# One core, a hybrid mLSTM and band attention trunk: column sums spread out, a weight split put behind the sums of the piece in front of it, one output group for all rows at once

## The chip, the cores and the metric

The kernel runs on one core of a Trainium2 chip. The metric is the device time of one execution in microseconds (us). Before the change the median of three runs is 2637.78 us (2635.75 to 2638.52).

## What is computed

One batch of 512 tokens of width 2048 goes through two layers. `mod` below is a product of a conditioning vector with wide matrices, one column at a time; the kernel makes each column by one pass over a 128x2048 tile (a "column sum", tile `ada`).

```python
# layer 1: mLSTM, 8 heads (q, k: 256 wide; v, o, z: 512 wide)
mod = silu(c) @ ada_w + ada_b                      # shift, scale, gate
h = rmsnorm(x) * (1 + scale) + shift
qk = silu(causal_conv(h @ w_qk))                   # 4 taps
v, o, z, gates = h @ w_v, h @ w_o, h @ w_z, h @ w_g + gate_b
ht = mlstm(q, k, v, log input gate, log forget gate)   # decays exp(...) times q k^T, times v
y = sigmoid(o) * rmsnorm(ht) * silu(z)
x = x + gate * rmsnorm(y @ a_w_out)
# shared keys and values, then layer 2: 16 heads of 128, band of 9 chunks of 64
k, v = (rmsnorm(x) * (1 + kscale) + kshift) @ kv_w
q, z = (rmsnorm(x) * (1 + scale) + shift) @ b_w_in
x = x + gate * rmsnorm((softmax(q k^T + bias) v * silu(z)) @ b_w_out)
```

## The kernel before

**Products.** All is float32. A product of two float32 tiles is made as three TensorE products of rounded halves: hi by hi, hi by lo, lo by hi (`mm3`, L314). Weights come from memory as one stream of pieces in the order of use, mostly 128x1024 (512 KB), into three tiles `wr` by SyncE's queue (`raw_load`, L253). Each piece is split into `wh`: hi is a cast on ScalarE, lo a subtraction on VectorE (`split`, L242, all on line L243). Three such pairs of tiles exist, so a split can be at most about two pieces ahead of TensorE.

**Seven products.** In the later parts two by two blocks are multiplied by seven products in place of eight (`proj_s`, L358, and `proj_v`, L422). For a piece this needs sums of its blocks: three VectorE instructions (L282, L283, L284; L283 writes into `wr` itself) make `ws`, which is split into `wsh` in the same way as `wh`. So such a piece costs VectorE three sums and two subtractions, and ScalarE two casts. `proj_v` makes the values of heads 3 to 7 (TensorE tiles `ps_dv`, `ps_cv`, `ps_av`, `ps_ev`; eight pieces each), the column groups 2 and 3 of the first half of `a_w_out`, and one group of the values of `kv_w`. The tile scheduler sets the order on each engine from priorities (`tc.high_priority`), and a small helper `behind` (L235) can force one instruction behind another on its engine.

**Stages.** The start and the columns needed first (0 to about 155 us); heads 0, 1 and 2 of the mLSTM; heads 3 to 7, each about 165 us, all alike; `a_w_out` in two halves of its rows; `kv_w`; 16 heads of the band attention; the last product. In heads 0 to 2 VectorE has 57 column sums to make besides its splits, scheduled by `background(n)` (L683): it sums the n oldest loaded tiles and refills up to three (two from one pool, one from another). Their 1 MB loads are issued by GpSimd's queue, which also carries the short row transfers `dsc` (`row_out`, L883) and the factors `f` of the heads. In `a_w_out`, further column sums ("whole", L1092 to L1103) are loaded by SyncE's queue between weight loads, two or three at a time.

**Head 0 to 2.** The convolution (`conv`, L787) works in 128x512 tiles tagged "t" of a pool of three, `tp`. Many others use this pool: `g32` of the gates, the squares `sq` of the norm (L1053), and the row that `row_out` sends to memory. The gates (`gates`, L747) are a chain of small VectorE steps that ends in `ssum` (L773), which TensorE waits for (`ps_at`, L782). The scores of a head (`scores`, L847) multiply `qk` tiles into `ps_s`, and multiply by decays that ScalarE makes with exp (L859, L861); silu of the convolution is L800. The two functions are in different tables of ScalarE, and a change of table is an instruction of its own, `ACT_TABLE_LOAD`.

**a_w_out, second half.** `rows(g, ms, ...)` makes column group g (512 columns) for the row blocks ms. Group 0 is made for all four row blocks of 128 tokens at once, groups 1 to 3 for two pairs of row blocks in turn, so that the weights of these groups are streamed twice. In the second pair the residual and the normed rows of the first pair are made (`residual`, `turned`, `key_inputs`).

**Band attention.** Eight pairs of k-tiles are multiplied by seven products, and their inputs need sums (`input_sums`, L1364, `three_sums`, L498), which VectorE makes before head 0 starts.

Of the kernel before, what the change touches and what calls it, by code (L numbers as in the profile page):

```python
# [29 lines left out]
SHIFTS = 9  # L30
# [17 lines left out]
ATT_PAIRS = 8  # L48
BANKS = ("pppp", "paaa")
# [54 lines left out]
def stream():  # L104
# [50 lines left out]
    tile_b("a_w_out", 0, KT)  # L155
    for _ in PAIRS:
        for g in range(1, 4):
# [8 lines left out]
    for h in range(BH):  # L166
        tile_s("b_w_in", h * P, D + h * P, ATT_PAIRS, True)
# [20 lines left out]
def hybrid_trunk(ctx, tc, xT, xN, c, adaT, cols, wst, wg, ext, kc, out):  # L188
# [73 lines left out]
    def wpiece(mat, groups=(), pl=None, bufs=(2, 2), early=False):  # L262
# [9 lines left out]
        with tc.high_priority(ahead[0]):  # L272
# [25 lines left out]
            parted[:] = split(hi, lo, raw, *first[1:] if i < 3 else ())  # L298
            out = [(hi, lo)]
            for j, t in enumerate(ts):  # L300
# [3 lines left out]
                split(sh, sl, t)  # L304
# [28 lines left out]
    def proj_a(mat, xs, ps, t0=0, t1=S):  # L333
        proj(mat, xs, [ps], 8, 0, len(xs), len(xs) - 1, t0, t1)
# [23 lines left out]
    def proj_s(mat, xs, ss, f, z1, z2, name, pl, bufs, at={}, merged=False, banks="pppp", lead=AHEAD):  # L358
# [4 lines left out]
        pieces = pair_pieces(f, merged)  # L363
        begun = set()
        h0, h1_ = slice(0, 256), slice(256, 512)
        for i, (sk, nk) in enumerate(pieces):
# [55 lines left out]
    def proj_v(mat, xs, ss, zs, name, pl, bufs, at={}):  # L422
# [41 lines left out]
        out = []  # L464
# [211 lines left out]
    loaded = []  # L676
# [6 lines left out]
    def background(n):  # L683
# [4 lines left out]
        while pending and len(loaded) < 3:  # L688
            p, bufs = (bp, 1) if len(pending) % 3 == 1 else (ap_, 2)
# [3 lines left out]
    for n, step in enumerate(steps):  # L693
        if n > len(steps) - 6:
# [38 lines left out]
    ahead[0] = AHEAD  # L733

# [12 lines left out]
    def gates():  # L747
# [4 lines left out]
        g32 = tp.tile([P, S], F32, tag="t", name="g32")  # L752
# [34 lines left out]
    def conv(ps, ch, name, lead, woven):  # L787

        acc = tp.tile([P, S], F32, tag="t", name=f"cv_{name}")
        with tc.high_priority(lead):  # L790
            if woven:
                rows = tp.tile([P, S], F32, tag="t", name=f"cu_{name}")
# [90 lines left out]
    def row_out(h, i, ps, f):  # L883

        r = tp.tile([P, S], F32, tag="t", name=f"row{h}_{i}")[0:1]
# [35 lines left out]
    for h in range(NH):  # L921
# [4 lines left out]
        for i in range(4):  # L926
# [6 lines left out]
            else:  # L933
                ps = newp(f"ps_qk{h}_{i}")
                proj_a("a_w_in", h1, ps)
            qk.append(conv(ps, chs[i], f"{h}_{i}", AHEAD if h == HALF else 100 if h > HALF and i > 1 else 0, h in (0, HALF)))
            if 1 < h <= HALF:
                background(2)
# [9 lines left out]
        if h == 0:  # L948
            background(2)
# [31 lines left out]
        for i in (2 * h, 2 * h + 1):  # L981
            pin(nc.sync.dma_start(bsc[i], ext[i].partition_broadcast(P)))
        if h == 0:
            for j in range(4):
# [14 lines left out]
        if h < HALF:  # L999
            background(2 + (h == 0))  # L1000
        if h:
            so = []
        for i in range(4):
# [26 lines left out]
        if h == 0:  # L1030
            background(2)
# [37 lines left out]
        if h < HALF:  # L1069
            background(3)  # L1070
# [107 lines left out]
    xrs = [[] for _ in range(4)]  # L1178
# [530 lines left out]
```

## Time and profile before

| what | value |
|---|---|
| median of three runs | 2637.78 us (2635.75 to 2638.52) |
| the profiled execution's own time | 2635.22 us |
| its span | 2633.4 us |
| mean clock granted to TensorE | 0.997 of full speed |
| TensorE (PE) busy | 2574.4 us, 98% |
| VectorE (DVE) busy | 2335.1 us, 89% |
| ScalarE (ACT) busy | 1428.7 us, 54% |
| moved by DMA | 510.62 MB, mean 194 GB/s |

The span runs from the first to the last recorded instruction; 1.8 us of the profiled execution's time lie around it. Busy TensorE time is not TensorE at its peak: the ends of its instructions are modelled, and they overlap. An idle time stands in brackets in the timeline, with what ended it behind the arrow.

### The profile page before, as it was taken

What the parts mean: (1) busy time and instruction counts of PE and PEld (TensorE: products, weight loads), DVE (VectorE), ACT (ScalarE), POOL (GpSimd) and SP (SyncE); (2) the same over time, 40 slices, a digit from 0 to 9 for tenths busy, and PEclk for the clock granted to TensorE, in tenths of its full rate; (3) what the DMA queues carried; (4) which work ended last, traced back from release to release, by engine and by line L of the source; (5) the groups of instructions that cost most, each with busy time, mean ns of one, the idle gap of its engine ahead of it and who ended that gap; (6) DMA issues with size and microseconds to landing.
All of it is one profiled execution on the core that took longest, in us unless ns stands there. A gap on an engine that the chain in (4) does not pass through costs nothing.

```text
span 2633.4 us, 45758 instructions
## 1 busy us (share of the span) xinstructions
PE 2574.4 (98%) x17994; PEld 2407.5 (91%) x17994; DVE 2335.1 (89%) x3812; ACT 1428.7 (54%) x2106; POOL 59.8 (2%) x118
## 2 busy tenths in 40 slices
PE   8999999999999999999999999999999999999998
PEld 6887787899999999999999898788999899999887
DVE  8978988999989999899998886977997999999767
ACT  4344533466555665556655453578543766776523
POOL 0000111000000000000000000000000000000000
PEclk9999999999999999999999999999999999999999
DMA  9876787533333333333336548988654544444787
GB/s 364 313 265 251 272 329 290 192 108 114 124 102 129 115 111 125 105 125 118 110 130 237 195 150 327 301 259 302 226 179 146 171 130 138 138 130 132 254 299 251
DMA packets 155315, 510.62 MB, mean 194 GB/s; under 512 B 17893, under 2 KB 31749, under 8 KB 140633
## 3 DMA queue, kind: packets, MB, share of 16 engines
q1 hardware_dynamic: 144346, 443.89, 49.6%
q0 software_dynamic: 10752, 63.79, 6.6%
q8 instruction: 141, 2.31, 0.4%
q14 instruction: 76, 0.62, 0.1%
HBM read 473.96 MB, written 38.90 MB: 195 GB/s over the span
## 4 chain that ended last, share of the span: by engine, by line
PE 56%; DVE 25%; DMA 8%; issue 7%; ACT 3%; POOL 0%; SPq 0%; DVEq 0%; ACTq 0%; POOLq 0%
DVE wh L243 6%; PE ps_y L311 5%; PE ps_azo L311 4%; PE ps_czo L311 4%; PE ps_dzo L311 4%; DVE ada L552 3%; PE ps_y_True L311 3%; PE ps_dz L311 3%; PE ps_cz L311 3%; PE ps_y_False L311 3%; PE ps_az L311 3%; DMA wr<-in_wst 3%; DVE wsh L243 2%; PE ps_bzo L311 2%; DVE cv L797 2%
## 5 line engine op out<-in xcount | busy, mean ns | idle before, releaser
L243 ACT CAST wh<-wr 128x1024 fp32r<-128x1024 f32 (+1 forms) x536 | 553.3, 1034 | 473.3 <-DVE wr L283 102.0
L243 DVE TENSOR_TENSOR wh<-wr,wh 128x1024 fp32r<-128x1024 f32 (+1 forms) x536 | 643.3, 1203 | 127.2 <-ACT wh L243 126.3
L243 ACT CAST wsh<-ws 128x768 fp32r<-128x768 f32 (+1 forms) x296 | 241.8, 817 | 298.4 <-PE ps_az L311 67.1
L243 DVE TENSOR_TENSOR wsh<-ws,wsh 128x768 fp32r<-128x768 f32 (+1 forms) x296 | 276.8, 935 | 45.7 <-ACT wsh L243 44.5
L552 DVE CUSTOM_DVE_ANT_0 ada<-ada,scB,cl 128x2048 f32<-128x2048 f32 (+1 forms) x89 | 205.8, 2322 | 11.3 <-DMA ada<-in_adaT 11.2
L282 DVE TENSOR_TENSOR ws<-wr 128x512 f32<-128x512 f32 (+1 forms) x296 | 198.5, 673 | 5.3 <-DMA wr<-in_wst 5.0
L311 PE MATMUL ps_y_False<-wh,y 128*128 128x512 f32 x768 | 168.6, 380 | 2.3 <-DVE wh L243 2.2
L311 PE MATMUL ps_y<-wh,y 128*128 128x512 f32 x768 | 168.6, 380 | 0.1
L311 PEld LDWEIGHTS ps_y_False<-wh,y 128*128 128x128 f32 x768 | 144.3, 189 | 24.4 <-DVE wh L243 4.2
L311 PEld LDWEIGHTS ps_y<-wh,y 128*128 128x128 f32 x768 | 144.3, 189 | 20.8 <-DVE wh L243 0.5
L311 PE MATMUL ps_kv<-wh,hkv 128*128 128x512 f32 x576 | 127.3, 381 | 1.6 <-DVE wh L243 1.5
L311 PE MATMUL ps_v<-wh,h 128*128 128x512 f32 x576 | 127.3, 380 | 0.0
L311 PEld LDWEIGHTS ps_kv<-wh,hkv 128*128 128x128 f32 x576 | 108.0, 189 | 18.5 <-DVE wh L243 3.3
L284 DVE TENSOR_TENSOR ws<-wr 128x256 f32<-128x256 f32 (+1 forms) x296 | 122.1, 414 | 3.1
L283 DVE TENSOR_TENSOR wr<-ws,wr 128x256 f32<-128x256 f32 (+1 forms) x296 | 121.8, 413 | 2.4
L311 PEld LDWEIGHTS ps_v<-wh,h 128*128 128x128 f32 x576 | 108.3, 189 | 15.8 <-issue 0.9
L311 PE MATMUL ps_l<-h,wh 128*128 128x512 f32 x480 | 107.7, 380 | 2.1 <-DVE wh L243 2.1
L311 PEld LDWEIGHTS ps_l<-h,wh 128*128 128x128 f32 x480 | 90.3, 189 | 16.5 <-DVE wh L243 3.3
L311 PE MATMUL ps_azo<-h,wh 128*128 128x256 f32 (+1 forms) x606 | 92.9, 285 | 0.0
L311 PE MATMUL ps_y_True<-wh,y 128*128 128x512 f32 x384 | 83.3, 379 | 0.0
L311 PEld LDWEIGHTS ps_y_True<-wh,y 128*128 128x128 f32 x384 | 72.5, 189 | 10.2
L311 PEld LDWEIGHTS ps_azo<-h,wh 128*128 128x128 f32 x606 | 79.2, 192 | 1.1
(431 smaller groups left out, 5825.2 us busy)
## 6 DMA issues: line engine op xcount, KB each, us to landing
wr<-in_wst SPq DMA_DIRECT2D x506, 512.0 KB, 3.7
ada<-in_adaT POOLq DMA_DIRECT2D x57, 1024.0 KB, 7.1
ada<-in_adaT SPq DMA_DIRECT2D x49, 1024.0 KB, 7.0
ada<-in_adaT SPq DMA_DIRECT2D x36, 512.0 KB, 6.5
wr<-in_wst SPq DMA_DIRECT2D x26, 384.0 KB, 6.2
xt<-nsc SPq DMA_DIRECT2D x32, 256.0 KB, 3.8
yr<-ysc SPq DMA_DIRECT2D x28, 256.0 KB, 5.4
ysc<-zo SPq DMA_DIRECT2D x24, 256.0 KB, 3.9
```

The source lines that it names most:

```text
L243: ins = nc.scalar.copy(hi, src), nc.vector.tensor_tensor(lo, src, hi.bitcast(F32), op=ALU.subtract)
L282: nc.vector.tensor_tensor(t[:, : 2 * w], r[:, w : 3 * w], r[:, : 2 * w], op=ALU.subtract)
L283: nc.vector.tensor_tensor(r[:, w : 2 * w], t[:, w : 2 * w], r[:, :w], op=ALU.add)
L284: nc.vector.tensor_tensor(t[:, 2 * w :], r[:, 3 * w :], r[:, w : 2 * w], op=ALU.subtract)
L311: product[0] = nc.tensor.matmul(ps, a, b, start=start, stop=stop)
L552: pin(nc.vector.tensor_tensor_reduce(c, c, (sc or scB)[:, j * w : (j + 1) * w], 1.0, mod[:, i : i + 1] if j else col(CB + i), ALU.mult, AL ...
L797: nc.vector.scalar_tensor_tensor(acc[:, d:], ps[:, : S - d], col(CW + 32 * (3 - d) + ch), acc[:, d:], op0=ALU.mult, op1=ALU.add)
```

## The change

The change has seven parts, and nothing else of the kernel is touched.

1. Three column sums fewer are made in heads 0 to 2 (`SHIFTS` 9 to 6); they are made in `a_w_out` with the others there.
2. `background` starts 12 steps before the end of the start and not 6, is called for one sum at a time, also between the two pieces of a projection (`mid`), and gets a fourth tile (`ring`) after the start.
3. For heads 0 to 2 a new pool `ep` gives the convolution, its input copy, `g32` and the row their own tiles, which were tiles of `tp`. The masked decays of head 0 are made behind its values.
4. The transfers of the attention's bias rows (`bsc`) are issued in heads 3 to 7 in place of all heads.
5. In `proj_v` the split of a piece's weights is put behind the splits of the sums of the piece in front of it, ScalarE's behind ScalarE's and VectorE's behind VectorE's (`chain`).
6. In the second half of `a_w_out` column group 1 is made for all four row blocks at once as well, so that eight weight pieces are streamed, cast and subtracted once less. The steps that hung on the three groups of the second pair hang on two.
7. Head 0 of the attention makes six of its eight pairs by seven products and the last two by eight (`ATT_FIRST`); the sums for these two are made in its steps 2 and 3, for the other heads. The products into B are made in two halves of 256 columns.

```diff
-SHIFTS = 9
+SHIFTS = 6
+ATT_FIRST = 6
...
-def pair_pieces(f, merged=False):
+def pair_pieces(f, merged=False, late=False):
...
+    if late:
+        out = [([[a]], [b]) for a, b in zip(sk[f - n :], nk)]
+        return [([sk[i : i + 2]], []) for i in range(0, f - n, 2)] + out
...
     tile_b("a_w_out", 0, KT)
+    tile_b("a_w_out", 512, KT)
     for _ in PAIRS:
-        for g in range(1, 4):
+        for g in range(2, 4):
...
-            parted[:] = split(hi, lo, raw, *first[1:] if i < 3 else ())
+            parted[:] = split(hi, lo, raw, *first[1:] if i < 3 else chain or ())
...
-                split(sh, sl, t)
+                done = split(sh, sl, t)
+                if chain is not None:
+                    chain[:] = done[::-1]
...
+            if mid and ka > k0:
+                mid()
             [(hi, lo)] = wpiece(mat)
...
-                        acc(ps, slice(0, S), main, b0 + 4 * m + 2 * j + t, xs[2 * k + j], False)
+                            for w in (h0, h1_) if late and t else (slice(0, S),):
+                                acc(ps, w, main, b0 + 4 * m + 2 * j + t, xs[2 * k + j][:, :, w], False)
...
-            held.append((k, *wpiece(mat, [2], pl, bufs)))
+            held.append((k, *wpiece(mat, [2], pl, bufs, chain=chain)))
...
-    loaded = []
+    loaded, ring = [], [(ap_, 2), (ap_, 2), (bp, 1)]
...
-        while pending and len(loaded) < 3:
-            p, bufs = (bp, 1) if len(pending) % 3 == 1 else (ap_, 2)
+        while pending and len(loaded) < len(ring):
+            p, bufs = ring.pop(0)
+            ring.append((p, bufs))
...
-        if n > len(steps) - 6:
+        if n > len(steps) - 12:
             background(2 if n % 2 else 0)
...
+    ep = mst.enter_context(pool("t0", side="right"))
+    ring.insert(0, (ep, 1))
...
+    def early_tile(h, tag, bufs, name):
+        return ep.tile([P, S], F32, tag=tag, name=name, bufs=bufs) if h else tp.tile([P, S], F32, tag="t", name=name)
...
-        acc = tp.tile([P, S], F32, tag="t", name=f"cv_{name}")
+        acc = early_tile(early, "cv", 3, f"cv_{name}")
...
-        r = tp.tile([P, S], F32, tag="t", name=f"row{h}_{i}")[0:1]
+        r = early_tile(h < HALF, "row", 2, f"row{h}_{i}")[0:1]
...
-                proj_a("a_w_in", h1, ps)
+                proj_a("a_w_in", h1, ps, lambda: background(1))
...
-        for i in (2 * h, 2 * h + 1):
+        for i in range(BH * (h - HALF - 1) // (NH - HALF - 1), BH * (h - HALF) // (NH - HALF - 1)) if h > HALF else ():
             pin(nc.sync.dma_start(bsc[i], ext[i].partition_broadcast(P)))
...
+    gate_row(0, 1)
+    rows(1, range(4), ys, whole_steps(3, (0, 2, 4, 6, 8, 10, 12)))
     for pair, ms in enumerate(PAIRS):
-        for g in range(1, 4):
+        for g in range(2, 4):
...
-                at = whole_steps(3, (0, 6, 12)) if g < 3 else whole_steps(3, (0,)) | {k: whole_sum for k in (4, 8, 12)}
+                at = whole_steps(3, (0, 6, 12)) if g < 3 else {k: whole_sum for k in (0, 4, 8)}
...
-                    w = slice(0, 256 + 256 * i)
+                    w = slice(0, S if k >= ATT_FIRST else 256 + 256 * i)
                     split(t[:, 0, w], t[:, 1, w], raw[i][:, w])
+                if k >= ATT_FIRST:
+                    plain[k] = raw
+                    h2s.append(None)
+                    continue
...
+    def plain_sums(k):
+        h2s[k] = three_sums(plain[k], kq, f"h2s{k}", ATT_PAIRS, h2[2 * k][:, :, 256:], True)
```

The scheduler turns this into another order of instructions on the engines. Three places follow, of before and of after the change apart. A name such as `wh116` is piece 116 of the weight stream, `ws116_0` its sums, `wsh116_0` the split of the sums; the last number of a name only tells tiles apart.

First place: VectorE in head 3, where the values begin. Rows of `wh` and `wsh` are the subtractions that make lo, `cv_3_2` and `cv_3_3` the convolution of head 3. Before:

```order
L284 TENSOR_TENSOR ws116_0_5471<-wr116_5469 128x256
L797 SCALAR_TENSOR_TENSOR cv_3_2_5270<-zq3_2_0_5033,cl_100,cv_3_2_5270 128x510
L797 SCALAR_TENSOR_TENSOR cv_3_3_5279<-zq3_2_1_5034,cl_100,cv_3_3_5279 128x510
L243 TENSOR_TENSOR wh116_5475<-wr116_5469,wh116_5475 128x1024
L243 TENSOR_TENSOR wsh115_0_5416<-ws115_0_5409,wsh115_0_5416 128x768
L797 SCALAR_TENSOR_TENSOR cv_3_2_5270<-zq3_2_0_5033,cl_100,cv_3_2_5270 128x509
L243 TENSOR_TENSOR wsh116_0_5478<-ws116_0_5471,wsh116_0_5478 128x768
```

After:

```order
L289 TENSOR_TENSOR ws116_0_5460<-wr116_5458 128x256
L813 SCALAR_TENSOR_TENSOR cv_3_2_5259<-zq3_2_0_5022,cl_100,cv_3_2_5259 128x510
L813 SCALAR_TENSOR_TENSOR cv_3_3_5268<-zq3_2_1_5023,cl_100,cv_3_3_5268 128x510
L248 TENSOR_TENSOR wsh115_0_5405<-ws115_0_5398,wsh115_0_5405 128x768
L248 TENSOR_TENSOR wh116_5464<-wr116_5458,wh116_5464 128x1024
L287 TENSOR_TENSOR ws117_0_5528<-wr117_5526 128x512
L248 TENSOR_TENSOR wsh116_0_5467<-ws116_0_5460,wsh116_0_5467 128x768
```

The subtraction of `wsh115_0` stood behind that of `wh116` and now stands ahead of it; a step of `cv_3_2` that stood between the two `wsh` is no longer there.

Second place: ScalarE at the same point of head 3. `cv_3_2` and `cv_3_3` with ACTIVATE are silu, `e3_0` is the first decay (exp), CAST makes hi. Before:

```order
L243 CAST wsh116_0_5478<-ws116_0_5471 128x768
L800 ACTIVATE cv_3_2_5270<-cv_3_2_5270 128x512
L243 CAST qk_3_2_5276<-cv_3_2_5270 128x512
L800 ACTIVATE cv_3_3_5279<-cv_3_3_5279 128x512
L243 CAST wh117_5543<-wr117_5537 128x1024
L243 CAST qk_3_3_5285<-cv_3_3_5279 128x512
L243 CAST wsh117_0_5546<-ws117_0_5539 128x768
L859 ACT_TABLE_LOAD
L859 ACTIVATE e3_0_5530<-nmd3_5289,aT_1513 128x128
```

After:

```order
L248 CAST wh117_5532<-wr117_5526 128x1024
L816 ACTIVATE cv_3_3_5268<-cv_3_3_5268 128x512
L875 ACT_TABLE_LOAD
L875 ACTIVATE e3_0_5519<-nmd3_5278,aT_1534 128x128
L248 CAST wsh117_0_5535<-ws117_0_5528 128x768
L816 ACT_TABLE_LOAD
L816 ACTIVATE cv_3_2_5259<-cv_3_2_5259 128x512
L248 CAST wh118_5601<-wr118_5595 128x1024
L248 CAST qk_3_2_5265<-cv_3_2_5259 128x512
L248 CAST qk_3_3_5274<-cv_3_3_5268 128x512
```

The two silu stood together ahead of the only table load in these rows. Now the first decay stands between them, so that the table is loaded once for exp and once more for silu, and the cast of `qk_3_2` stands behind both loads and behind the casts of `wh117`, `wsh117_0` and `wh118`.

Third place: VectorE at the end of the start. `ada32` to `ada35` are column sums (ISA is the sum's instruction, the row with `mod` alone reads its accumulator), `q1_0` to `q1_3` take products of head 1 out of TensorE's banks. Before:

```order
L243 TENSOR_TENSOR wh32_1203<-wr32_1125,wh32_1203 128x768
L524 SCALAR_TENSOR_TENSOR h1_15_1314<-h1t_15_1315,mod_103,h1_15_1314 128x512
L243 TENSOR_TENSOR gw_1519<-graw_1518,gw_1519 128x16x16
L731 TENSOR_TENSOR q1_0_265<-q1_0_265,ps_l6_6_1183 128x512
L243 TENSOR_TENSOR wh33_1228<-wr33_1153,wh33_1228 128x768
L731 TENSOR_TENSOR q1_1_266<-q1_1_266,ps_l7_6_1208 128x512
L243 TENSOR_TENSOR wh34_1256<-wr34_1181,wh34_1256 128x768
L243 TENSOR_TENSOR wh35_1284<-wr35_1206,wh35_1284 128x768
```

After:

```order
L742 TENSOR_TENSOR q1_0_265<-q1_0_265,ps_l6_6_1189 128x512
L562 ISA ada32_0_1178,mod_103<-ada32_0_1178,scB_123,cl_100 128x2048
L562 ISA mod_103 128x1
L562 ISA ada33_0_1180,mod_103<-ada33_0_1180,scB_123,cl_100 128x2048
L562 ISA mod_103 128x1
L742 TENSOR_TENSOR q1_1_266<-q1_1_266,ps_l7_6_1220 128x512
L248 TENSOR_TENSOR wh33_1240<-wr33_1153,wh33_1240 128x768
L248 TENSOR_TENSOR wh34_1274<-wr34_1187,wh34_1274 128x768
L562 ISA ada34_0_1182,mod_103<-ada34_0_1182,scB_123,cl_100 128x2048
L562 ISA mod_103 128x1
L562 ISA ada35_0_1211,mod_103<-ada35_0_1211,scB_123,cl_100 128x2048
```

Before, the first column sum behind `wh32` came behind `wh38`; now six of them, `ada32` to `ada37`, stand between `wh32` and `wh37`, the first four of them in these rows.

More of the change, by code (lines that the diff above doesn't have):

```diff
@@ L260, in raw_load, with wpiece @@
         loads.append(raw)
-    def wpiece(mat, groups=(), pl=None, bufs=(2, 2), early=False):
+    def wpiece(mat, groups=(), pl=None, bufs=(2, 2), early=False, chain=None):
         if stock and not early:
@@ L356, in proj_b, with proj_s @@
             held.clear()
-    def proj_s(mat, xs, ss, f, z1, z2, name, pl, bufs, at={}, merged=False, banks="pppp", lead=AHEAD):
+    def proj_s(mat, xs, ss, f, z1, z2, name, pl, bufs, at={}, merged=False, banks="pppp", lead=AHEAD, late=False):
         D, C, A, B = [(newa if b == "a" else newp)(f"ps_{n}{name}") for n, b in zip("dcab", banks)]
-        pieces = pair_pieces(f, merged)
+        pieces = pair_pieces(f, merged, late)
         begun = set()
@@ L462, in empty @@
             return z0, z1
-        out = []
+        out, chain = [], []
         for k in range(n):
@@ L1176, in row_rstd @@
         return r
-    xrs = [[] for _ in range(4)]
+    xrs, fetched_xr = [[] for _ in range(4)], [0] * 4
     def fetch_xr(m, n):
-        for g in range(len(xrs[m]), len(xrs[m]) + n):
-            xrs[m].append(xr_p.tile([P, S], F32, tag="xr", name=f"xr{m}_{g}"))
+        for g in range(fetched_xr[m], fetched_xr[m] + n):
+            if m < 3:
+                xrs[m].append(xr_p.tile([P, S], F32, tag="xr", name=f"xr{m}_{g}"))
+            else:
+                if g % 2 == 0:
+                    t = kp.tile([P, 2, S], F32, tag="k", name=f"xr{m}_{g}", bufs=KT)
+                    xrs[m] += [t[:, i, :] for i in range(2)]
             nc.sync.dma_start(xrs[m][g], xN[m, :, g * S : (g + 1) * S])
+        fetched_xr[m] += n
     def residual(m):
@@ L1393, in hybrid_trunk @@
         for g in range(2):
-            turn = {2 + 6 * i: lambda i=i: turned(1, [i], True) for i in range(3)} if pair == 0 and g == 1 else {}
+            turn = {k: lambda i=i: turned(1, [i], True) for i, k in enumerate((4, 8, 14))} if pair == 0 and g == 1 else {}
             if pair == 0 and g == 0:
@@ L1459, in queries @@
         z2 = at.tile([P, 2, 256], F32, tag="z", name=f"z{h}", bufs=2)
-        proj_s("b_w_in", h2, h2s, ATT_PAIRS, z1, z2, f"z{h}", kq, (2, 2), steps, True)
+        proj_s("b_w_in", h2, h2s, ATT_PAIRS if h else ATT_FIRST, z1, z2, f"z{h}", kq, (2, 2), steps, True, late=True)
         zq, sz = (z.rearrange("p a t -> p (a t)") for z in (z1, z2))
@@ L1551, in hybrid_trunk @@
         if h < BH:
-            qs[h], szs[h] = queries(h, {1: turn, 2: mid, 3: end})
+            steps = {1: turn, 2: mid, 3: end}
+            if h == 0:
+                add_at(steps, {2 + i: lambda k=k: plain_sums(k) for i, k in enumerate(plain)})
+            qs[h], szs[h] = queries(h, steps)
+            if h == 0:
+                for k, raw in plain.items():
+                    s1 = h2s[k][0]
+                    split(s1[:, 0, :], s1[:, 1, :], raw[0][:, 256:])
+                tst.close()
         else:
```

59 lines of the change are left out of this document (29 added, 30 removed).

## The prediction

> **What bounds the kernel now.** I read the page first: busy times, then its costliest groups. TensorE is busy for almost the whole span.
>
> ```profile
> PE 2574.4 (98%) x17994; PEld 2407.5 (91%) x17994; DVE 2335.1 (89%) x3812; ACT 1428.7 (54%) x2106; POOL 59.8 (2%) x118
> ...
> L243 ACT CAST wh<-wr 128x1024 fp32r<-128x1024 f32 (+1 forms) x536 | 553.3, 1034 | 473.3 <-DVE wr L283 102.0
> L243 DVE TENSOR_TENSOR wh<-wr,wh 128x1024 fp32r<-128x1024 f32 (+1 forms) x536 | 643.3, 1203 | 127.2 <-ACT wh L243 126.3
> ...
> L311 PE MATMUL ps_y_False<-wh,y 128*128 128x512 f32 x768 | 168.6, 380 | 2.3 <-DVE wh L243 2.2
> ```
>
> The change takes no product away (head 0 of the attention even gets a few more), so it can only take away time in which TensorE waits. The waits of TensorE by what ended them are the budget; these are the rows that the change can touch, out of some 50 us in all.
>
> ```profile
> PE ps_cv L311 <- DVE wsh L243: 9.8, 10, 1.6
> PE ps_q L311 <- ACT sp_q L243: 4.9, 5, 3.8
> PE ps_s L311 <- ACT qk L243: 4.4, 1, 4.4
> PE ps_z L311 <- DVE wh L243: 3.4, 2, 2.7
> ...
> PE ps_y_False L311 <- DVE wh L243: 2.2, 4, 0.8
> ...
> PE ps_dz L311 <- DVE h2s L243: 1.8, 1, 1.8
> PE ps_dz L311 <- ACT h2s L243: 1.7, 1, 1.7
> ...
> PE ps_n L311 <- DVE so L1054: 1.3, 1, 1.3
> ...
> PE ps_at L782 <- DVE ssum L773: 1.2, 1, 1.2
> ```
>
> The columns are the total, the number of waits and the longest. The sum of these rows is 30.7 us, so no version of this change gains much more. The view counts from the modelled end of the last matmul, and that lies late: one of 512 columns is recorded as 380 ns (the page's last row above), but twelve in a row take 2.75 us, so the first and the last start 2.75 less 0.38 us apart, 0.215 us for each.
>
> ```profile
> 161.42 2.75 PE L311 MATMUL ps_lead<-h,wh 128*128 128x512 f32 x12
> ```
>
> So each wait really costs about 0.16 us more than its row. A measurement of this kernel can tell about 0.2%, 5.3 us, from no change.
>
> **Heads 0 to 2 (parts 1 to 3).** Three places wait here, and the timeline shows why. At 315 us the scores of head 1 wait for `qk`, because its convolution began late: ScalarE waited for a row's transfer to give back a tile of `tp`, and VectorE then had column sums between its steps.
>
> ```profile
> 293.79 0.81 ACT L795 ACTIVATE cv<-q,cl 128x512 f32<-128x512 f32 x1 [1.57 <-DMA dsc<-row]
> ...
> 315.09 1.14 PE L311 MATMUL ps_s<-qk,qk 128*128 128x512 f32 x2 [4.37 <-ACT qk L243]
> ...
> 378.90 2.35 DVE L552 CUSTOM_DVE_ANT_0 ada<-ada,scB,cl 128x2048 f32<-128x2048 f32 x1 [2.16 <-DMA ada<-in_adaT]
> ...
> 420.22 0.60 ACT L1053 ACTIVATE sq<-ps_n 128x512 f32<-128x512 f32 x1 [5.69 <-DMA dsc<-row]
> ```
>
> The waits of the stretch from 600 to 1420 us alone tell how much of `ps_q` belongs to later heads:
>
> ```profile
> PE ps_q L311 <- ACT sp_q L243: 1.1, 4, 0.3
> ```
>
> With its own tiles the convolution of head 1 is done long before, ahead of the gates, so the 4.4 us go. What is late next there is `f0`, which waits for GpSimd's transfers, 0 to 2 us of it uncovered; I take 0. Around 385 us `ps_z` waits 3.4 us because VectorE waits for loads of sums; the fourth tile and three sums fewer (3 x 2.35 = 7.1 us of VectorE) should cover that. At 423 us the row's transfer held a tile that `sq` needed for 5.69 us, and TensorE paid 3.8 of it and 1.3 in `ps_n`; rows now have tiles of their own. Together 3.4 + 3.8 + 1.3 = 8.5 us, with 5 as the low end, since sums still crowd there.
>
> Against it stands what these sums displace. They now come first between `wh32` and `wh37`, into time in which VectorE sits idle waiting for TensorE or ScalarE:
>
> ```profile
> 155.77 0.89 DVE L243 TENSOR_TENSOR wh<-wr,wh 128x768 fp32r<-128x768 f32 x1
> ...
> 161.62 0.69 DVE L731 TENSOR_TENSOR q<-q,ps_l 128x512 f32<-128x512 f32 x1 [2.01 <-PE ps_l L311]
> ...
> 166.37 0.96 DVE L243 TENSOR_TENSOR wh<-wr,wh 128x768 fp32r<-128x768 f32 x1 [2.88 <-ACT wh L243]
> 169.39 0.69 DVE L731 TENSOR_TENSOR q<-q,ps_l 128x512 f32<-128x512 f32 x1 [2.06 <-PE ps_l L311]
> ...
> 228.52 0.74 DVE L773 SCALAR_TENSOR_TENSOR ssum<-ps_li,cl,gate_nmd 8x512 f32<-8x512 f32 x1
> ...
> 311.82 0.74 DVE L797 SCALAR_TENSOR_TENSOR cv<-q,cl,cv 128x509 f32<-128x509 f32 x1
> ```
>
> And from the view of the transfers, with the median time to landing at the end:
>
> ```profile
> ada<-in_adaT POOLq DMA_DIRECT2D x57, 1024.0 KB, 7.1
> ```
>
> `wh32` is split at 156.7 and TensorE takes it up at 161.4: a lead of 4.7 us, and two sums are 4.7 us. Pieces behind follow at 18 x 0.215 = 3.9 us, in which VectorE has 1.6 us of other work (a split of 0.9 and one step of 0.7), so the lead grows again by 2.3 us with each piece that has no sum in front of it. It falls to about 1 us or nothing at `wh33` and `wh35`, and is made good by `wh41`. This covers the sums if their loads land in the usual 7.1 us; if each of the three pairs lands 2 us later, TensorE loses 3 x 2 = 6. I take 0.7, with 0 to 6. At the gates, nine convolution steps of head 1 (0.74 us each, 0.66 less their overlap) now stand in front of `ssum`: 6 us more of VectorE's work in that stretch, of which some goes into places where the chain of the gates waits for ScalarE. The wait of 1.2 us becomes about 3: +1.8, between 0 (all of it in such places) and 4. Heads 0 to 2: -4.4 - 8.5 + 0.7 + 1.8 = -10.4.
>
> **Heads 3 to 7 (parts 4 and 5).** Each head waits twice for a `wsh`. The first time, VectorE subtracted `wh116`, which TensorE needed only at 649.63, ahead of `wsh115`, for which TensorE stood idle.
>
> ```profile
> 643.48 1.22 DVE L243 TENSOR_TENSOR wh<-wr,wh 128x1024 fp32r<-128x1024 f32 x1
> 644.62 0.95 DVE L243 TENSOR_TENSOR wsh<-ws,wsh 128x768 fp32r<-128x768 f32 x1
> ...
> 645.62 0.49 PE L311 MATMUL ps_cv<-wsh,h1s 128*128 128x256 f32 x2 [1.56 <-DVE wsh L243]
> ...
> 649.63 0.50 PE L311 MATMUL ps_dv<-wh,h1s 128*128 128x256 f32 x3
> ...
> 654.32 1.46 PE L311 MATMUL ps_s<-qk,qk 128*128 128x512 f32 x6
> ```
>
> The swap saves 644.62 - 643.48 = 1.14 us, and the second wait (9.8 / 5 - 1.56 = 0.4) goes too: 1.54 a head, 7.7 in five. `wh116` then still has 3 to 4 us of lead. But the chain also moves ScalarE, as the second place of the order shows: a load of the table and the first decay come between the two silu, and another load before the second.
>
> ```profile
> 650.38 0.83 ACT L243 CAST wsh<-ws 128x768 fp32r<-128x768 f32 x1
> 651.23 1.28 ACT L859 ACT_TABLE_LOAD   x1
> 652.53 0.40 ACT L859 ACTIVATE e<-nmd,aT 128x128 f32<-128x128 f32 x1
> ```
>
> A switch costs 651.21 to 652.53, 1.32 us. From the page, the means of VectorE's sums and subtractions:
>
> ```profile
> L243 DVE TENSOR_TENSOR wsh<-ws,wsh 128x768 fp32r<-128x768 f32 (+1 forms) x296 | 276.8, 935 | 45.7 <-ACT wsh L243 44.5
> L282 DVE TENSOR_TENSOR ws<-wr 128x512 f32<-128x512 f32 (+1 forms) x296 | 198.5, 673 | 5.3 <-DMA wr<-in_wst 5.0
> ...
> L283 DVE TENSOR_TENSOR wr<-ws,wr 128x256 f32<-128x256 f32 (+1 forms) x296 | 121.8, 413 | 2.4
> ```
>
> An instruction overlaps the one in front of it by 0.08 (643.48 + 1.22 to 644.62). In the new order VectorE does, from 643.48 on, `wsh115`, `wh116`, the first sum of piece 117, `wsh116` and the second sum: 0.86 + 1.14 + 0.59 + 0.86 + 0.33 = 3.8, so that `wh117` can be cast from 647.3. From there ScalarE has, in its new order and less overlaps: that cast 0.95, silu 0.55, load 1.3, exp 0.35, cast of `wsh117` 0.8, load 1.3, silu 0.55, cast of `wh118` 0.95, cast of `qk_3_2` 0.6: 7.35 us, to 654.7. TensorE stands at `ps_s` at 654.32 - 1.14 = 653.2. So a wait takes the place of the one removed: 1.5 us a head, 7.5 in five. Net -0.2, between -7.7 (the silu get ahead of the decay after all) and +4 (0.8 a head more).
>
> The Trainium skill ("ScalarE: Activation LUTs", section "What ACT_TABLE_LOAD costs") gives 1283 ns for the load and about 1380 ns for a drain, some 2.66 us for a switch to another set. This case's trace agrees on the load, 1.28 us, and disagrees on the switch, where the next function starts 0.02 us behind the load. By the page the two switches would delay `qk_3_2` by 2 x 1.34 = 2.7 us more a head, an estimate by which the sum would be 13.4 us higher.
>
> The bias rows (part 4) are 16 transfers spread over heads with idle DMA; nothing.
>
> **a_w_out (part 6).** Eight pieces fewer are loaded, cast and subtracted, in a stretch where TensorE has only 2.6 us of work for 512 KB (two row blocks, 12 x 0.215). The 2.2 us of `ps_y_False` should go where group 1 is concerned and remain in groups 2 and 3 of the first pair; I take -2.0, between 0 and -2.2. The work of the second pair's group 1 is pressed into groups 2 and 3, where ScalarE was half free: +0.7, between 0 and 2. Three more "whole" sums are hidden under group 1, whose pieces give TensorE 5.2 us each.
>
> **Attention (part 7).** Head 0 starts late for the last input sums:
>
> ```profile
> 2092.53 0.38 PE L311 MATMUL ps_dz<-h2s,wh 128*128 128x256 f32 x1 [1.68 <-ACT h2s L243]
> 2094.68 0.79 PE L311 MATMUL ps_dz<-h2s,wh 128*128 128x256 f32 x2 [1.77 <-DVE h2s L243]
> ```
>
> With two pairs by eight products these sums are due a head later: -3.5. The products cost 1536 columns more, three times 0.215: +0.6.
>
> **The sum.** -10.4 - 0.2 - 2.0 + 0.7 - 3.5 + 0.6 = -14.8; some eleven waits that go add 11 x 0.16 = 1.8: -16.6. The profiled execution took 2635.22, so its like would be 2618.6. The median lies 2.56 above the profiled execution; put on the median, 2637.78 - 16.6 = 2621.2, say 2621.
>
> **The rivals.** First, *the chain works as drawn*: the new wait for `qk` does not come, since the silu are ready ahead of the decay. For it: the trace before has them in that order; against: the new order is fixed in the program. Then 7.5 less, 2613.5.
>
> Second, *the front gives half of it back*: loads of the sums landing 2 us late at `wh33` to `wh37` (+5.3 over my 0.7) and the gates at +4 (2.2 over my 1.8). For it: VectorE is the engine with least slack beside TensorE, and its sums waited for loads here before (the 2.16 at 378.90). Then 2621 + 7.5 = 2628.5.
>
> Third, *a table switch between two others costs twice the 1.32 us of the row*: two of them stand ahead of `qk_3_2`, so the new wait is 2 x 1.3 = 2.6 us longer in each of five heads. Then 2621 + 13 = 2634, no change that can be told. The row speaks against it, but it has one switch, with none close behind. This is what that page of the Trainium skill would make of it.
>
> Fourth, on the other side, *the chain puts the splits in series*. In `proj_v` VectorE has 0.67 + 0.41 + 0.41 + 1.20 + 0.94 = 3.6 us a piece; TensorE has 649.63 to 654.32, 4.7 us. If VectorE's subtractions wait each time for ScalarE's casts of `wsh` and then `wh` in turn (0.83 + 1.03), the piece takes 5.5 us, 0.8 more than TensorE's. Over the 56 chained pieces (eight uses of `proj_v` of eight pieces, less the first of each) that is 45 us: 2666. It begins where VectorE waits over 1.1 us a piece; slower by over 5.3 us it gets from 28 such pieces on (22 us). Against it: in the new order the first sum of the next piece fills the place between the two subtractions, and ScalarE is busy for only 54%.
>
> That the chain isn't met is excluded by the first place of the order.
>
> **How the numbers follow.** Forecast 0.48 (2621; 2615 to 2627 by the bounds of its small terms), first rival 0.16, second 0.23, third 0.07, fourth 0.06. So faster 0.48 + 0.16 + 0.23 = 0.87, same 0.07, slower 0.06. The range from 2610 to 2632 holds the first three cases with most of their spread; the third and fourth rivals, 0.13, lie outside.
>
> **What would show it.** Right: no wait of `ps_s` near 315 and none of `ps_q` near 423; `ps_at` at some 3 us; `ps_cv` waits of about 0.4 in heads 3 to 7, and in their place five waits of `ps_s` for `qk` of about 1.5; none of `ps_dz`. Wrong: `ps_s` waits in heads 3 to 7 absent (first rival) or 4 us long (third), waits of TensorE for `wh` at 160 to 190 (second), or `ps_dv` waiting for `wh` in the values (fourth).

## The result and the profile after

The change is faster. Its median is 2620.74 us (six runs, 2618.11 to 2624.05) against 2637.49 us of the kernel before in the same sessions (six runs, 2632.24 to 2643.02); the ratio is 0.9936 with a 95% interval of 0.9922 to 0.9950, 13 to 21 us less. The forecast was 2621. The profiled execution took 2619.10 us (span 2617.3), so the two traces compared here lie 16.1 us apart.

First the busy times on the page of the changed kernel, then TensorE's waits by what ended them (total, number, longest):

```profile
PE 2570.9 (98%) x17988; PEld 2404.7 (92%) x17988; DVE 2324.1 (89%) x3804; ACT 1430.5 (55%) x2106; POOL 57.9 (2%) x115
```

```profile
PE ps_s L318 <- ACT qk L248: 7.6, 5, 1.5
PE ps_kv L318 <- DVE wh L248: 2.4, 6, 0.7
PE ps_gg L841 <- DVE ggate L839: 2.4, 1, 2.4
PE ps_x L1246 <- DVE hkv L248: 2.2, 2, 1.9
...
PE ps_cv L318 <- DVE wsh L248: 2.1, 5, 0.4
PE ps_li L318 <- ACT g L766: 2.1, 1, 2.1
PE ps_cz L318 <- DVE z L422: 1.9, 1, 1.9
...
PE ps_x L1246 <- DVE xn L1238: 1.4, 2, 0.8
...
PE ps_at L795 <- DVE ssum L786: 0.6, 1, 0.6
...
PE ps_y_False L318 <- DVE wh L248: 0.3, 1, 0.3
```

All rows of this view add up to 48.9 us in 50 waits before and to 36.3 us in 49 now. The waits of `ps_z`, `ps_n` and `ps_dz` are gone, and of `ps_q` only the 1.1 us of heads 3 to 7 are left; five new ones of `ps_s` and longer single ones of `ps_li`, `ps_cz` and `ps_x` have come. The waits fell by 12.6 us, and TensorE's busy time, 2574.4 us before, by the other 3.5. There the clock has changed. The view of stretches has the clock granted to TensorE in the third column from the right; these are three stretches of 4 us, before:

```profile
2092.00:2096.00 4.00, 1.69 (x7) 1.50 (x8) 4.00 (x9) 2.17 (x3) 0.00 (x0) 0.69 0.40 126
2096.00:2100.00 4.00, 4.00 (x21) 4.00 (x21) 3.95 (x7) 0.46 (x2) 0.00 (x0) 0.50 0.15 45
315.00:319.00 4.00, 3.91 (x13) 3.43 (x14) 4.00 (x8) 3.95 (x6) 0.53 (x1) 0.57 0.44 140
```

and one of 5 us after:

```profile
213.00:218.00 5.00, 5.00 (x12) 2.78 (x11) 5.00 (x6) 4.27 (x6) 0.00 (x0) 0.66 0.00 0
```

Behind the wait at 315 and the two at 2092 and 2094 the clock was halved for some microseconds. Counted in slices of 5 us (one less the clock, times 5), and without the last 20 us of the span, in which TensorE hardly works, the slower clock cost 5.1 us before (1.7 at 315, 3.4 at 2090 to 2105) and 1.7 us after (at 210 to 220). So 12.6 us of waits and 3.4 us of clock make 16.0 of the 16.1 us. The added products, 0.6 us by the forecast, should have taken as much away again, so that some 0.7 us stay unexplained. The clock differs not in these two profiles alone: over the six executions of the change its mean is 0.9977, over 17 of the kernel before (in the session of e9 to e11) 0.9965, and 0.0012 of 2620 us is 3.1 us, an estimate.

One execution of e9 below ran in a slow state (3237.72 us at a mean clock of 0.767) and is left out of its figures.

### The profile page after: what moved, and what is told of

It is laid out like the page before. It is cut to its first block, busy times and chain, and to the rows that moved or that the text cites. A ratio compares the mean times of both kernels' runs of the same rounds, so it can differ in the third digit from the quotient of the medians.

```text
span 2617.3 us, 45696 instructions
## 1 busy us (share of the span) xinstructions
PE 2570.9 (98%) x17988; PEld 2404.7 (92%) x17988; DVE 2324.1 (89%) x3804; ACT 1430.5 (55%) x2106; POOL 57.9 (2%) x115
## 5 line engine op out<-in xcount | busy, mean ns | idle before, releaser
L248 ACT CAST wh<-wr 128x1024 fp32r<-128x1024 f32 (+1 forms) x528 | 544.8, 1033 | 462.4 <-DVE wr L288 110.2
L248 DVE TENSOR_TENSOR wh<-wr,wh 128x1024 fp32r<-128x1024 f32 (+1 forms) x528 | 635.7, 1207 | 120.0 <-ACT wh L248 119.3
L562 DVE CUSTOM_DVE_ANT_0 ada<-ada,scB,cl 128x2048 f32<-128x2048 f32 (+1 forms) x86 | 198.9, 2322 | 3.5 <-DMA ada<-in_adaT 3.5
```

The costliest lines, as they stand in the source:

```text
L248: ins = nc.scalar.copy(hi, src), nc.vector.tensor_tensor(lo, src, hi.bitcast(F32), op=ALU.subtract)
L562: pin(nc.vector.tensor_tensor_reduce(c, c, (sc or scB)[:, j * w : (j + 1) * w], 1.0, mod[:, i : i + 1] if j else col(CB + i), ALU.mult, AL ...
```

## The experiments

Each experiment changes the changed kernel unless its text says otherwise. Ratios are to the kernel before in the same session; the change itself has 0.9936.

### e1: without the chain

```diff
-            held.append((k, *wpiece(mat, [2], pl, bufs, chain=chain)))
+            held.append((k, *wpiece(mat, [2], pl, bufs)))
```

> The change without its part 5: no split is put behind another in proj_v. Theory (the chain only exchanges one wait for another): in heads 3 to 7 TensorE's waits for wsh come back to 9.8 us in ten waits and the 7.6 us of ps_s for qk go, so the time stays at 2621 within 2 us (the ratio to the kernel before near 0.9936). Rival (the chain is a cost by itself, through its two table loads more a head): 2613. Rival (the chain is a gain, its new wait comes from something else): 2629, with ps_s waits still there.

Measured: 2619.12 us, ratio 0.9931 (0.9916 to 0.9946). TensorE's waits without the chain:

```profile
PE ps_cv L318 <- DVE wsh L248: 9.7, 10, 1.6
```

No row of `ps_s` for `qk` is left. With the chain heads 3 to 7 have 7.6 + 2.1 = 9.7 us of these waits, without it 9.7 us. The chain, one of the three parts that the title names, exchanges one wait for another to the tenth of a microsecond; the waits gain nothing by it, and the times of the two kernels can't be told apart.

### e2: both silu ahead of the decays

```diff
-            silu[0] = nc.scalar.activation(acc, acc, AF.Silu)
+            silu[:] = silu[1], nc.scalar.activation(acc, acc, AF.Silu)
...
-                behind(ins, silu[0])
+                for s in silu:
+                    behind(ins, s)
```

> The change with one more ordering: in heads 3 to 7 the decays are put behind both of the last two silu and not behind the later one of the program alone, so that ScalarE loads its tables once a head less each way (111 loads in place of 121). Theory (the wait of ps_s is the table switches between the two silu): the five waits of 1.5 us go or shrink under 0.3, the waits for wsh stay at 0.4 a head, and the time falls by 6.5 to 8.5 us, to about 2613. Rival (ScalarE's queue is late there anyway, through the casts of wh117 and wsh117): waits of 1 us stay, 2618. Rival (a switch takes 2.66 us): a fall of over 12 us.

To see what e2 takes away, first the changed kernel: ScalarE's timeline in head 4, and TensorE's row at the same place.

```profile
798.21 0.63 ACT L816 ACTIVATE cv<-cv 128x512 f32<-128x512 f32 x1
798.85 1.28 ACT L875 ACT_TABLE_LOAD   x1
800.15 0.40 ACT L875 ACTIVATE e<-nmd,aT 128x128 f32<-128x128 f32 x1
800.46 0.82 ACT L248 CAST wsh<-ws 128x768 fp32r<-128x768 f32 x1
801.29 1.28 ACT L816 ACT_TABLE_LOAD   x1
802.59 0.63 ACT L816 ACTIVATE cv<-cv 128x512 f32<-128x512 f32 x1
803.12 1.03 ACT L248 CAST wh<-wr 128x1024 fp32r<-128x1024 f32 x1
804.06 1.13 ACT L248 CAST qk<-cv 128x512 fp32r<-128x512 f32 x2
...
804.72 0.70 PE L318 MATMUL ps_s<-qk,qk 128*128 128x512 f32 x2 [1.52 <-ACT qk L248]
```

These are the steps of the prediction behind the cast of `wh117`, in its order and at its durations: from the first silu at 798.21 to the casts of `qk`, between them two loads of the table. A load between two others takes 1.28 us and the next instruction starts 0.02 us behind it, as where it stood alone.

Measured: 2619.89 us, ratio 0.9934 (0.9919 to 0.9948). The wait of `ps_s` is gone as expected, but the time did not fall, which neither theory had: TensorE waits for `wsh` again, later in the same head. All five waits of `ps_s` together are gone, 7.6 us, but 6.1 us came up here.

```profile
PE ps_cv L318 <- DVE wsh L248: 8.2, 10, 1.2
```

In head 3 of e2 this is VectorE and TensorE at the end of the values:

```profile
652.42 1.23 DVE L248 TENSOR_TENSOR wh<-wr,wh 128x1024 fp32r<-128x1024 f32 x1 [0.35 <-ACT wh L248]
653.56 0.42 DVE L884 SCALAR_TENSOR_TENSOR e<-ps_s,e 128x256 f32<-128x256 f32 x1
653.89 0.95 DVE L248 TENSOR_TENSOR wsh<-ws,wsh 128x768 fp32r<-128x768 f32 x1
...
654.90 0.49 PE L318 MATMUL ps_cv<-wsh,h1s 128*128 128x256 f32 x2 [1.20 <-DVE wsh L248]
```

The first row is the piece of the next projection, the third the last sums of the values, for which TensorE stands. Before, the same order cost 0.40 us a head, and none in the changed kernel, only because TensorE came 1.5 us late from `ps_s`. e5 and e6 ask whether the order or the amount of VectorE's work is the cause.

### e3: heads 0 to 2 with the shared tiles

```diff
-        return ep.tile([P, S], F32, tag=tag, name=name, bufs=bufs) if h else tp.tile([P, S], F32, tag="t", name=name)
+        return tp.tile([P, S], F32, tag="t", name=name)
```

> The change with its part 3 undone: convolution, its copy, g32 and rows of heads 0 to 2 take tiles of tp again; the rest of the change stays. Theory (the two large waits of heads 1 and 2 came from tiles of tp that came free late): waits of ps_s of some 4 us near 315 and of ps_q of some 4 us near 420 come back, the time rises by 8 to 9 us, to 2629. Rival (fewer sums and the fourth tile removed them): no wait over 1 us there, 2621.

Measured: 2622.18 us, ratio 0.9945 (0.9925 to 0.9964). The waits of TensorE from 190 to 430 us:

```profile
PE ps_s L318 <- DVE e L883: 2.2, 1, 2.2
PE ps_li L318 <- ACT g L766: 2.0, 1, 2.0
PE ps_s L318 <- ACT qk L248: 1.0, 2, 0.7
PE ps_at L795 <- DVE ssum L786: 0.9, 1, 0.9
```

This lies between my two theories. Some 3 us of `ps_s` come back, not 4 and 4, and no wait of `ps_q`. Only 1.0 us of it is for `qk`, as I had argued; the 2.2 us are for VectorE's `e`, ahead of which VectorE had waited 2.53 us for a transfer (`ssum` from `dsc`). With the sums spread out, a row's tile no longer holds up `ps_q`, even where the tiles are shared. In all of the profile e3 waits 35.4 us, the change 36.3, so what part 3 adds to the other parts isn't shown.

### e4: eight pairs by seven products

```diff
-ATT_FIRST = 6
+ATT_FIRST = 8
```

> The change with its part 7 undone in head 0 of the attention: eight pairs by seven products again, the two halves of B only where a pair is made by eight. Theory: the waits of ps_dz for the input sums come back with 3.5 us, the wait of ps_cz for z (1.9 us) goes, 0.6 us of products go: 2622, 1 us more. Rival (the wait of ps_cz comes from banks that are emptied late, whatever the number of sevens): it stays, 2624.

Measured: 2622.70 us, ratio 0.9943 (0.9925 to 0.9961). The two waits of `ps_dz` are back:

```profile
PE ps_dz L318 <- ACT h2s L248: 1.8, 1, 1.8
...
PE ps_dz L318 <- DVE h2s L248: 1.8, 1, 1.8
```

and that of `ps_cz` is gone: 3.6 against 1.9 us and 0.6 of products. In these profiles the clock adds to it: behind the pair of waits it was at 0.5 to 0.6 for 4 us and more, behind the single wait of the changed kernel at 1.00. That is no rule: behind the same single wait it was 0.64 over 4 us in e5 and 0.57 in e12. The two places make 1.7 us more of waits, all waits of e4 (37.1 us) only 0.8 more than in the change. The time went the way that I expected, but the two intervals overlap.

### e5 and e6: the chain carried over the end, and VectorE's scalings moved

e5 is e2 with the chain handed on (`left`); e6 is e5 with the scalings of the head in front moved (`tail[0]` is the subtraction of the last sums' split).

```diff
-            parted[:] = split(hi, lo, raw, *first[1:] if i < 3 else chain or ())
+            parted[:] = split(hi, lo, raw, *first[1:] if i < 3 else chain or left)
+            left.clear()
...
+        left[:] = chain
         for z, e in zip(out, (h0, h1_)):
```

> The kernel of e2 (decays behind both silu) with the chain carried over the end of proj_v: the split of the next projection's first piece is put behind the last sums' split as well. In e2 VectorE subtracted that first piece (1.2 us) right ahead of the last wsh of the values, and TensorE waited 1.2 us for it in each head. Theory A (each wait is an order of two subtractions, and the chain stops one piece too early): these waits shrink to about 0.1 a head, all waits for wsh in heads 3 to 7 from 8.2 to about 2.5, the time falls by 5 to 6 us against e2, to about 2614. Theory B (VectorE is full in this stretch, so that the waits come to the same sum wherever they fall): a wait of about 1 us a head appears at another place, the time stays at 2620.

```diff
-                behind(ins, parted[0])
+                behind(ins, tail[0] if h >= HALF else parted[0])
...
-            add_at(at, {6: head_due})
+            add_at(at, {14: head_due})
```

> The kernel of e5 with VectorE's four scalings of the head in front (0.7 us each) moved from the middle of the values to behind their last wsh. Theory A: nothing is left to gain there, as e5 within 2 us, about 2614. Theory B: 2.4 us of VectorE's work leave the full stretch, so that only here the waits go; 2613, while e5 stays at 2620.

Measured: e5 2619.54 us, ratio 0.9920 (0.9905 to 0.9934); e6 2618.64 us, ratio 0.9920 (0.9906 to 0.9933). Waits of e5 in heads 3 to 7, 610 to 1420 us, and then of e6:

```profile
PE ps_cv L319 <- DVE wsh L248: 3.6, 10, 0.4
...
PE ps_czo L319 <- DVE wsh L248: 2.3, 5, 0.5
```

```profile
PE ps_czo L320 <- DVE wsh L248: 2.1, 5, 0.4
PE ps_cv L320 <- DVE wsh L248: 2.1, 5, 0.4
```

The 8.2 us of e2 became 3.6, and 2.3 came up at the first product of the next projection: 5.9 us, where the changed kernel has 9.7. So each theory has a half of it: 4.6 us went with the order (theory A), and half of them came back behind (theory B, 0.5 us a head where I expected 1). In e6 it is 4.4 us with 0.2 of `ps_dzo`, though 2.4 us of VectorE's work a head had left the stretch. Neither kernel reached the 2614 or 2613 of its theory. The gain of 3.8 us of waits against the changed kernel is not seen clearly in the times: the intervals of e5 and of the change overlap.

### e7 and e8: the tiles alone, and the change without the spread

e7 is the kernel before with the pool `ep` and `early_tile` alone, without the later decays of head 0. e8 is the change with three tiles in the ring, the 6 steps, and the calls of `background` as they were; the diff shows some of these lines.

```diff
-        if n > len(steps) - 12:
+        if n > len(steps) - 6:
...
-    ring.insert(0, (ep, 1))
...
-                proj_a("a_w_in", h1, ps, lambda: background(1))
+                proj_a("a_w_in", h1, ps, None)
```

> The kernel before with part 3 alone: its own tiles for convolution, copies, g32 and rows in heads 0 to 2. As I argued in the prediction (late tiles made the waits at 315 and 423): ps_s near 315 (4.4) and ps_q near 423 (3.8) go, ps_z near 385 (3.4) stays; 2629. Rival, after e3 (the spread of the sums removed them): a wait of some 4 us stays at one of the two places or moves right behind it; 2634 to 2638.

> The change with part 2 undone: three tiles for column sums, two sums at a time, begun 6 steps before the end of the start, no sums between the two pieces of a projection; six sums and own tiles stay. As I argued: ps_z waits near 385 come back in part (2 to 3 us), no waits of ps_s and ps_q; the wait of ps_li for g32 at the gates (2.1 us) goes; about 2621. Rival (the spread is what brings the gain in heads 0 to 2): waits of over 6 us in all between 315 and 430; 2628.

Measured: e7 2626.40 us, ratio 0.9948 (0.9929 to 0.9967); e8 2626.15 us, ratio 0.9948 (0.9934 to 0.9961). Waits from 190 to 430 us of e7, and then of e8:

```profile
PE ps_z L311 <- DVE wh L243: 4.4, 4, 1.5
PE ps_at L783 <- DVE ssum L774: 1.9, 1, 1.9
PE ps_o L311 <- DVE wh L243: 1.2, 1, 1.2
PE ps_s L311 <- DVE qk L243: 0.9, 1, 0.9
```

```profile
PE ps_z L318 <- DVE wh L248: 3.0, 2, 1.6
PE ps_at L794 <- DVE ssum L785: 1.9, 1, 1.9
PE ps_s L318 <- DVE qk L248: 1.6, 1, 1.6
PE ps_o L318 <- DVE wh L248: 1.5, 1, 1.5
```

e7 goes with what I had argued: the tiles alone take away `ps_q` (0.3 left) and most of `ps_s`, and `ps_z` stays. Its four executions lie 11 us apart, and the profiled one is the fastest. In e8 `ps_z` stays in part and `ps_li` is gone, as argued, but `ps_s` waits 1.6 us and `ps_o` 1.5, and the time lies nearer to the rival's 2628 than to my 2621; by the ratios it is 3 us more than the change, with intervals that overlap. The waits of this stretch are 15.3 us before, 9.3 with the tiles alone, 8.0 without the spread, 6.1 without the tiles (e3) and 2.9 with all. Either part takes away `ps_q`; `ps_z` goes with the spread (e3 has none) and not with the tiles; of `ps_s` each leaves a part, and only the two together take it all but for 0.2.

### e9: column group 1 per pair again

```diff
-    tile_b("a_w_out", 512, KT)
     for _ in PAIRS:
-        for g in range(2, 4):
+        for g in range(1, 4):
...
-    rows(1, range(4), ys, whole_steps(3, (0, 2, 4, 6, 8, 10, 12)))
```

> The change with its part 6 undone: column group 1 of the second half of a_w_out per pair of row blocks again, eight weight pieces more, the steps of the second pair on three groups; the 22 sums of a_w_out are spread over its steps. Theory (part 6 gives at one place what it takes at another): ps_y_False waits 2 us again instead of 0.3, the wait of ps_x for hkv (1.9 to 2.4 us, in all runs with part 6) falls to 0.5, TensorE's waits between 1580 and 2000 us stay at 7 to 8 us in all, the time stays within 2 us of the change: 2621. Rival (eight pieces fewer are worth their ScalarE and VectorE work): 2624 or more, with 3 us more of waits.

Measured: 2630.75 us (eleven executions), ratio 0.9972 (0.9960 to 0.9984), slower than the change by 0.0036, some 9 us. The waits from 1580 to 2000 us in e9:

```profile
PE ps_y_False L317 <- DVE wh L247: 3.5, 2, 3.0
PE ps_x L1245 <- DVE hkv L247: 1.3, 2, 1.0
PE ps_y_False L317 <- ACT wh L247: 1.2, 1, 1.2
PE ps_x L1245 <- DVE rsn L1192: 1.1, 1, 1.1
```

In the time the rival is right. In the waits of the profile the theory is nearer: 8.3 us here and 7.7 in the change, and in the profiles the whole way from the second half of `a_w_out` to the attention took 498.6 us before, 499.3 in the change and 500.2 in e9, 1.7 of these by the clock. But the profiled execution, 2622.47 us, is the fastest of the eleven, so it does not show what made the others slow. Their mean clock of 0.9966, against 0.9977, would make some 3 us, an estimate; the rest of the 9 us is open. The longest wait here is partly of my making, since with 22 sums to place VectorE waited for one of them ahead of the weights:

```profile
1651.93 2.35 DVE L561 CUSTOM_DVE_ANT_0 ada<-ada,scC,cl 128x2048 f32<-128x2048 f32 x1 [3.62 <-DMA ada<-in_adaT]
```

So in this arrangement the stretch has no room for the three more sums without part 6. What part 6 would be worth with 19 sums wasn't tried.

### e10: nine sums in heads 0 to 2

```diff
-SHIFTS = 6
+SHIFTS = 9
...
-    rows(1, range(4), ys, whole_steps(3, (0, 2, 4, 6, 8, 10, 12)))
+    rows(1, range(4), ys, whole_steps(3, (0, 4, 8, 12)))
```

> The change with its part 1 undone: nine shift columns are summed in heads 0 to 2 again, three fewer in a_w_out, with the fourth tile and the spread as in the change. Theory (the spread makes room for them): waits of TensorE between 190 and 610 us grow by less than 2 us; 2621 to 2623. Rival (the three sums, 7.1 us of VectorE, are what the gain in heads 0 to 2 comes from): 5 us or more of waits there; 2626.

Measured: 2621.38 us, ratio 0.9938 (0.9921 to 0.9955). In heads 0 to 2 this wait of head 2 grew, from 0.4 us, and 0.2 us of `ps_q` came:

```profile
PE ps_czo L318 <- DVE wsh L248: 2.1, 2, 1.6
```

The spread makes room for these sums; moving three of them is worth 2 us of waits, and nothing that the times show.

### e11 and e12: the gates

e11 is e5 with the first step of head 1's convolution behind the copy of `g32`; e12 is e5 with idle products in the place of the wait.

```diff
+            if early and not woven:
+                behind(ins, taken[0])
```

> The kernel of e5 with one more ordering: the first step of head 1's convolution on ScalarE is put behind the copy of g32, which TensorE waits for at the gates (2.1 us in the change, with the granted clock at 0.7 in the 4 us behind it). Theory: that wait falls under 0.5 us and the clock stays at 1.00 there; ps_at stays under 1.5; so 2 to 4 us less than e5, 2612 to 2616. Rival (the gates' chain is late by VectorE, and the wait only moves to ps_at): ps_at rises to 2 or 3 us, the time stays as e5.

```diff
+        for _ in range(9):
+            mm(bank(ps_i, S), ones_r, walk(h1[0][:, 0, :], S), True, True)
         mm(ps_i[:8], sel[:, 0:8], g32[:32], True, True)
```

> The kernel of e5 with nine idle products (216 ns each) on TensorE between the gates' product and the product that waits for g32; their result is overwritten. In e5 TensorE waited 2.3 us there, and the granted clock was 0.50 to 0.7 in the 5 us from 215 us on, as in five of the seven other profiles with this wait. Theory (a wait of some 2 us lowers the clock for the 3.4 us behind it, a cost of about 1.7 us beside the wait): with the wait filled the clock is 1.00 in all of 200 to 230 us, ps_li waits under 0.6 us, and the time is as e5 or up to 2 us less, 2613 to 2616 in the profile. Rival (the clock falls there for another reason, such as the small products of the gates): the clock is under 0.9 in 213 to 222 us as before.

Measured: e11 2619.21 us, ratio 0.9929 (0.9913 to 0.9944); e12 2620.59 us, ratio 0.9930 (0.9914 to 0.9946). In e11 the wait of `ps_li` is gone and that of `ps_at` is 1.9 us in place of 0.6:

```profile
PE ps_at L799 <- DVE ssum L790: 1.9, 1, 1.9
```

This is the rival: VectorE sets the end of this chain. The clock did not stay at 1.00 either; it fell behind the new wait, to 0.57 from 234 to 238 us. In e12 the wait is down to 1.22 us, and the clock from 215 to 220 us is 0.66 as in e5; this is e12:

```profile
215.00:220.00 5.00, 5.00 (x14) 3.31 (x13) 5.00 (x7) 3.61 (x6) 0.00 (x0) 0.66 0.00 0
```

The products shortened the wait but did not fill it, so e12 does not show that the clock falls there without a wait; it shows that 1.1 us less of waiting did not keep it up. The profiled execution took 2626.42 us, not the 2613 to 2616 of the theory, with three such stretches of slower clock. No kernel of this study is clearly faster than the change.

## Why the prediction was right

**Heads 3 to 7: right, but for one price.** Forecast: 7.7 us of waits for `wsh` go but for a rest, five waits of 1.5 us for `qk` come, net -0.2. The profile has 2.1 left and 7.6 come, net -0.1. The row of ScalarE's order is what told it; e1 shows that the chain brings nothing. I gave no reason why the second wait of 0.4 us a head should go. By e2 it goes because TensorE comes late from `ps_s`: without that delay it is 1.2 us. So the price of my first rival, 7.5 us, was wrong too: e2 has no wait of `ps_s` for `qk` and still 8.2 us for `wsh`, only 1.5 us less than the change.

**Heads 0 to 2: right in sign, too small.** Forecast -10.4. From 190 to 610 us the waits fell from 15.3 + 2.2 = 17.5 to 3.3 us, by 14.2. The terms of `ps_s`, `ps_z`, `ps_q` and `ps_n` (-12.9) came but for 0.2. What I had taken for costs was smaller or elsewhere: the sums between `wh32` and `wh37` cost TensorE nothing (1.5 us of waits from 130 to 190 us before and after, so the 0.7 was 0), head 2 lost 1.8 us more of waits than I counted, and the rows of `ps_d` and of `ps_n` for `row` another 1.0. The gates cost 1.3 in place of 1.8, but not where I put it: the wait is for ScalarE's copy of `g32`, and that stood behind two steps of head 1's convolution.

```profile
210.44 0.81 ACT L811 ACTIVATE cv<-q,cl 128x512 f32<-128x512 f32 x1
211.44 0.81 ACT L811 ACTIVATE cv<-q,cl 128x512 f32<-128x512 f32 x1 [0.19 <-DVE qk L248]
212.16 0.56 ACT L766 COPY g<-ps_g 32x512 f32<-32x512 f32 x1
```

**a_w_out: the step that failed.** I took -2.0 for `ps_y_False` and +0.7 for the work pressed into two groups, -1.3 in all. The -1.9 came. Behind it, from 1580 to 2000 us, the waits rose from 6.5 to 7.7 us, in the rows of `ps_x` (+1.2), `ps_dk` (+1.0) and `ps_kv` (+0.9). So the term was mis-sized by 2.4 us, +3.1 in place of +0.7. I take it that `turned` and the inputs of the keys now meet in fewer steps, since `ps_x` waits 1.88 us for `hkv`; with three groups again (e9) this wait is 0.96 us and that of `ps_kv` is gone, but e9 moves sums as well, so the reason is argued and not shown.

**Attention: the gain came, with a wait behind it.** The 3.5 us went. I named nothing that is late next, and it was `z`, on VectorE, for which `ps_cz` waits 1.9 us; the term is -1.6 in place of -3.5.

**The ends of matmuls: no such term.** I added 1.8 us for eleven waits fewer. There are 49 in place of 50, so nothing was due; whether a wait costs 0.16 us more than its row wasn't tested. In its place stands the clock, 3.4 us, of which I had said nothing although the page of the kernel before has a mean of 0.997. That the total fits to a microsecond is in part luck: the misses in heads 0 to 2 and the clock (-3.8 and -3.4) meet those of `a_w_out`, attention, the ends of matmuls and a later `ps_gg` (+2.4, +1.9, +1.8 and +0.8); smaller rows add some 1.3, and the 0.7 of the first section lies on the other side.

**The rivals.** The first (no new wait of `ps_s`) is out by the five rows of it. The second (late loads at `wh33` to `wh37`) did not happen. The third, a switch of table at double price, is out by the timeline of e2's section: two loads close together, each followed by the next function after 0.02 us. The Trainium skill's 2.66 us for a switch ("ScalarE: Activation LUTs", section "What ACT_TABLE_LOAD costs") is not what this trace shows; its 1283 ns for the load is. The fourth (splits in series) is out too: no wait of `ps_dv` for `wh` appeared.

## What to carry to other kernels

When an order is forced on one engine, read what the scheduler then does on the others: here the two subtractions were put right on VectorE, and ScalarE's switch of tables took the gain back. A wait that goes uncovers the one behind it (`wsh` behind `ps_s` in e2, `ps_at` behind `ps_li` in e11, `z` behind the input sums), so what is late next belongs into the sum with a price. Two parts that each take away the same wait cannot be added up: with the tiles alone (e7) and in the change without them (e3) the gain was 0.0052 and 0.0055, with both 0.0064. Each has an interval of 0.0014 to 0.0019 to either side, so it is the sum of the two that is excluded, and no order among the three is shown.

## What the runs showed of the hardware

The clock granted to TensorE falls to one half for about 3.4 us at a time, or for twice that, and each 3.4 us cost 1.7. Leaving out the first 100 and the last 20 us, in the ten profiles up to e8 it did so within 4 us of 12 of the 32 waits of 1.8 us or more, and of 4 of the 78 waits from 1.0 to 1.8 us. In all fourteen profiles each of these stretches begins in a wait of 1.2 us or more or within 3 us behind one, but most such waits have none. The Trainium skill ("TensorE: Matmul & The Clock Gate", section "Part 1: The HAM clock gate") has a gate that halves the clock after an idle window of some 3.4 us that runs freely. The two states and the 3.4 us agree; that a single wait of 2 us can be enough, and that shortening one to 1.22 us (e12) did not help, the passage on the gate does not say. Whether the wait or the small products around it makes the clock fall is left open. The change's executions differ by some 6 us, and their mean clock by 0.002, which is 5 us of the span. Such dips are a part of that scatter: over the 17 executions of the kernel before named above, 0.001 less of mean clock goes with 2.7 us more of time, where 0.001 of the span is 2.6, with a correlation of -0.65. The rest of the scatter is open.
